# Nineteen weight units whose low part is completed by an accumulating DMA instead of a VectorE subtraction

## The chip, the cores and the metric

The kernel runs on one core of a Trainium2 chip. The metric is device time in microseconds, the median of several executions. Engines: PE (TensorE matmul), PEld (its weight loads), DVE (VectorE), ACT (ScalarE), POOL (GpSimd) and SP (SyncE), which issues nearly all DMAs.

## What is computed

One layer of a hybrid decoder trunk on 512 tokens of width 2048, all in float32:

```
h    = rms_norm(x, norm1_g)
proj = h @ w_in            # columns: aq ak av | bu bg | cq ck cv
out_a = dilated mixture of attentions (8 heads x 64)         from aq, ak, av
out_b = silu(layer_norm(causal depthwise conv(bu * sigmoid(bg))))
out_c = sliding-window grouped-query attention with sinks (16 heads x 64) from cq, ck, cv
x    = x + concat(out_a, out_b, out_c) @ w_out
h2   = rms_norm(x, norm2_g)
x    = x + (silu(h2 @ w_gate) * (h2 @ w_up)) @ w_down
```

q and k are normalised per head before the attentions.

## The kernel before

**Matmuls in three parts.** A float32 operand is split into a high part, rounded to the fp32r type, and a low part, the operand less its high part, in fp32r too. A product is then three matmuls that add up in PSUM (`mm3`, lines 321 to 324): high weights by high activations (322), high weights by low activations (323), low weights by high activations (324). Activations are kept as pairs `hh`, `hl`; weights as pairs `wh`, `wl`.

**Weight units.** Weights arrive in units of 128 partitions by 1024 columns (512 KB). The input projection takes units 0 to 62: units 0 to 10 belong to the first four projections, worked together, and from unit 11 on each further projection of the list `PROJ` takes two units, an odd one and then an even one (`project`). Units 63 to 94 are `w_out`; the FFN follows with other blocks. A unit's 8 slices of 128 columns take 24 matmuls of 512 columns.

**From the raw unit to the pair.** `pump` issues the loads on SP (line 243) into a few raw buffers, in order, as they come free. `next_unit` is called when a unit's matmuls are about to be written down; it calls `split_up_to(u + 2)`, so a unit is split two units ahead of its use. In the projections the split is a cast on ACT (line 289, raw to `wh`) and a subtraction on DVE (line 263, raw less `wh` gives `wl`). The subtraction is not written down at once but kept in the list `lows` and written down after the fourth slice of the unit in progress (`lows_now` in `project`). `wh` and `wl` have three buffers each (`SPLIT_BUFS`), so the cast of unit u waits until PE has read the high part of unit u-3 for the last time, which is about when unit u-2 begins.

**Release of raw buffers.** While the projections run (`cooling`), a raw buffer that was split goes to the list `cool`; `lows_now` moves the lists on (`release`) and calls `pump`, but only where `lows` holds something. A buffer is thus given back one and a half units after its split.

**The work around it.** Everything beside the projections' matmuls (convolution, heads' normalisation, attention) is placed by a hand-made clock: `ticks.tick()` is called after every second slice, and each step is due some ticks after the one before. Instructions of an engine run in the order in which they are written down, each waiting for what it reads. POOL's queue in this stage holds, among others: the product of the gated linear unit (line 573), the power steps that make the scales of q and k (lines 664 to 666), the scaling of v by the norm (773), and the triangular masks that spread the attention's turned probabilities, high and low (`spread_out`, lines 906 and 909, tiles `c..ph` and `c..pl`). PE reads those masks' results in `weigh` (lines 974 and 975). ACT's queue holds, besides the casts of the weights, the exponentials, the copies of PSUM and the high parts of activations (for example `c..hp`, line 892, and `av`, line 779); DVE's the taps of the convolution (582), the low parts and the reductions.

## Time and profile before

| | |
|---|---|
| median of 3 runs | 1841.37 us (1841.23 to 1842.32) |
| profiled execution | 1840.9 us, span 1839.1 us, granted PE clock 1.00 |
| busy: PE, PEld, DVE, ACT, POOL | 1832.4, 1522.4, 1428.2, 1312.8, 1018.3 us |
| DMA | 337.81 MB, mean 184 GB/s, queue q1 takes 62.3% of 16 engines |
| stage with the changed units | 100 to 345 us of the span |

The profile is one execution. Times in its rows are from the start of the span. A row of the timeline has start, duration, engine, line, operation, the tile written and the tiles read (buffer numbers left out), the shape, and in brackets how long the engine had been idle and what ended that. A PE duration is modelled and overlaps the next one; matmuls of 512 columns start about 0.23 us apart. DMA issues show on the issuing engine's queue (SPq).

### The profile page before, as it was taken

What the parts mean: (1) busy time and instruction counts of PE and PEld (TensorE: products, weight loads), DVE (VectorE), ACT (ScalarE), POOL (GpSimd) and SP (SyncE); (2) the same over time, 40 slices, a digit from 0 to 9 for tenths busy, and PEclk for the clock granted to TensorE, in tenths of its full rate; (3) what the DMA queues carried; (4) which work ended last, traced back from release to release, by engine and by line L of the source; (5) the groups of instructions that cost most, each with busy time, mean ns of one, the idle gap of its engine ahead of it and who ended that gap; (6) DMA issues with size and microseconds to landing.
All of it is one profiled execution on the core that took longest, in us unless ns stands there. A gap on an engine that the chain in (4) does not pass through costs nothing.

```text
span 1839.1 us, 26573 instructions
## 1 busy us (share of the span) xinstructions
PE 1832.4 (100%) x8319; PEld 1522.4 (83%) x8319; DVE 1428.2 (78%) x2024; ACT 1312.8 (71%) x1784; POOL 1018.3 (55%) x793
## 2 busy tenths in 40 slices
PE   9999999999999999999999999999999999999998
PEld 7888888888888888888888888888888888888887
DVE  7689888986689877777777777777777777777777
ACT  6355644553468788888888888888887778877775
POOL 0126544110003557886888767887776558776552
PEclk9999999999999999999999999999999999999999
DMA  7353255453343466777867777677687579877635
GB/s 277 89 149 122 88 144 156 111 174 120 132 138 106 113 162 182 206 206 185 223 177 211 207 185 224 175 205 208 182 271 258 199 233 283 266 255 258 237 120 109
DMA packets 401612, 337.81 MB, mean 184 GB/s; under 512 B 185408, under 2 KB 327872, under 8 KB 401472
## 3 DMA queue, kind: packets, MB, share of 16 engines
q1 hardware_dynamic: 400896, 335.33, 62.3%
q8 instruction: 66, 1.08, 0.3%
q10 hardware_dynamic: 576, 0.79, 0.1%
q14 instruction: 74, 0.61, 0.1%
HBM read 261.61 MB, written 66.03 MB: 178 GB/s over the span
## 4 chain that ended last, share of the span: by engine, by line
PE 99%; DVE 1%; DMA 0%; issue 0%; SPq 0%; ACT 0%; DVEq 0%
PE out L1315 15%; PE out L1313 15%; PE out L1316 15%; PE out L1578 7%; PE out L1579 7%; PE out L1580 7%; PE o L324 3%; PE o L323 3%; PE o L322 3%; PE cq L322 2%; PE cq L324 2%; PE cq L323 2%; PE aq L322 1%; PE ak L322 1%; PE av L322 1%; PE aq L324 1%
## 5 line engine op out<-in xcount | busy, mean ns | idle before, releaser
L1313 PE MATMUL out<-wh,h 128*128 128x512 f32 x1232 | 479.2, 389 | 0.0
L1315 PE MATMUL out<-wl,h 128*128 128x512 f32 x1232 | 479.2, 389 | 0.0
L1316 PE MATMUL out<-wh,h 128*128 128x512 f32 x1232 | 479.2, 389 | 0.0
L1313 PEld LDWEIGHTS out<-wh,h 128*128 128x128 f32 x1232 | 231.3, 188 | 48.0
L1316 PEld LDWEIGHTS out<-wh,h 128*128 128x128 f32 x1232 | 231.3, 188 | 48.0
L1315 PEld LDWEIGHTS out<-wl,h 128*128 128x128 f32 x1232 | 231.3, 188 | 47.8
L1578 PE MATMUL out<-wh,a 128*128 128x512 f32 x620 | 240.4, 388 | 0.0
L1579 PE MATMUL out<-wl,a 128*128 128x512 f32 x620 | 240.3, 388 | 0.0
L1580 PE MATMUL out<-wh,a 128*128 128x512 f32 x620 | 240.3, 388 | 0.0
L289 ACT CAST wh<-w 128x1024 fp32r<-128x1024 f32 (+2 forms) x94 | 96.9, 1031 | 138.6 <-PE o L323 49.3
L1588 DVE TENSOR_TENSOR y<-y,out 128x512 f32<-128x512 f32 x192 | 128.3, 684 | 45.4 <-PE out L1580 43.8
L263 DVE TENSOR_TENSOR wl<-w,wh 128x1024 fp32r<-128x1024 f32 (+2 forms) x95 | 114.3, 1204 | 33.5 <-ACT wh L289 33.2
L1578 PEld LDWEIGHTS out<-wh,a 128*128 128x128 f32 x620 | 116.4, 188 | 24.0
L1579 PEld LDWEIGHTS out<-wl,a 128*128 128x128 f32 x620 | 116.4, 188 | 23.8
L1580 PEld LDWEIGHTS out<-wh,a 128*128 128x128 f32 x620 | 116.4, 188 | 23.8
L582 DVE SCALAR_TENSOR_TENSOR y<-bu,cst,y 128x511 f32<-128x511 f32 (+14 forms) x120 | 89.7, 747 | 1.1
L322 PE MATMUL o<-mh_c,wh 128*128 128x512 f32 x128 | 51.0, 399 | 0.0
L322 PE MATMUL cq<-hh,wh 128*128 128x512 f32 x128 | 50.3, 393 | 0.0
L324 PE MATMUL o<-mh_c,wl 128*128 128x512 f32 x128 | 50.0, 391 | 0.0
L323 PE MATMUL o<-ml_c,wh 128*128 128x512 f32 x128 | 50.0, 390 | 0.0
L323 PE MATMUL cq<-hl,wh 128*128 128x512 f32 x128 | 49.9, 390 | 0.0
L324 PE MATMUL cq<-hh,wl 128*128 128x512 f32 x128 | 49.9, 390 | 0.0
(2357 smaller groups left out, 4741.5 us busy)
## 6 DMA issues: line engine op xcount, KB each, us to landing
od<-a SPq DMA_DIRECT2D x154, 256.0 KB
a<-od SPq DMA_DIRECT2D x154, 256.0 KB
w<-in_wi SPq DMA_DIRECT2D x58, 512.0 KB
w<-in_wo SPq DMA_DIRECT2D x32, 512.0 KB
x<-in_xT SPq DMA_DIRECT2D x16, 256.0 KB
xr<-in_xT SPq DMA_DIRECT2D x16, 256.0 KB
x2d<-xr SPq DMA_DIRECT2D x16, 256.0 KB
z<-x2d SPq DMA_DIRECT2D x64, 64.0 KB
```

What stands on the lines that cost most here:

```text
L263: fn(*args)
L289: (nc.vector.tensor_copy if u == 0 else nc.scalar.copy)(hi[:, :n], t[:, :n])
L322: nc.tensor.matmul(out, wh, xh, start=start, stop=False)
L323: nc.tensor.matmul(out, wh, xl, start=False, stop=False)
L324: nc.tensor.matmul(out, wl, xh, start=False, stop=stop)
L1313: nc.tensor.matmul(b, x[:, high], wh[:, s], start=c == f == 0 and q in (7, 1, 5, 2), stop=False, skip_group_check=True)
L1315: nc.tensor.matmul(b, x[:, high], wl[:, s], start=False, stop=False, skip_group_check=True)
L1316: nc.tensor.matmul(b, x[:, low], wh[:, s], start=False, stop=c == f == 1, skip_group_check=True)
L1578: nc.tensor.matmul(b[:, lo:hi], x[:, high], wh[:, s], start=start, stop=False, skip_group_check=True)
L1579: nc.tensor.matmul(b[:, lo:hi], x[:, high], wl[:, s], start=False, stop=False, skip_group_check=True)
L1580: nc.tensor.matmul(b[:, lo:hi], x[:, low], wh[:, s], start=False, stop=last, skip_group_check=True)
L1588: getattr(eng, op)(t, t, src)
```

## The change

For the units of a fixed set, every second one from 21 to 57 (which is 19 units: the first half of each projection from cq1 to aq2 in the order of `PROJ`), the subtraction on DVE is left out. ACT writes the negative of the raw unit, rounded to fp32r, into `wl` right after the cast into `wh`; then a DMA issued from POOL's queue reads the unit from DRAM once more and adds it to `wl` in place. The sum is the raw unit less its high part, as before. The list `lows` gets no entry for such a unit, so nothing is written down for it after the fourth slice, and the release of raw buffers and the loads that follow it happen there only for the other units. Where `lows` is empty after the split, `next_unit` calls `pump` itself.

```
+LOWS_BY_DMA = set(range(21, 58, 2))
...
+    def complete(lo, u, n):
+        nc.gpsimd.dma_start(lo[:, :n], units[u], accum_op=ALU.add)
...
                 (nc.vector.tensor_copy if u == 0 else nc.scalar.copy)(hi[:, :n], t[:, :n])
-                lows.append((eng.tensor_sub, lo[:, :n], t[:, :n], hi[:, :n].bitcast(F32)))
+                if u in LOWS_BY_DMA:
+                    nc.scalar.activation(lo[:, :n], t[:, :n], AF.Copy, scale=-1.0)
+                    complete(lo, u, n)
+                else:
+                    lows.append((eng.tensor_sub, lo[:, :n], t[:, :n], hi[:, :n].bitcast(F32)))
                 if not late_lows:
                     lows_now()
```

## Prediction

> **What bounds the kernel now.** I read the head of the page first, then the chain that ended last, then the engines' busy times over the stage that the change touches (100 to 345 us), and last the waits of the PE instructions that read what other engines made there.

> ```profile
> span 1839.1 us, 26573 instructions
> ...
> PE 1832.4 (100%) x8319; PEld 1522.4 (83%) x8319; DVE 1428.2 (78%) x2024; ACT 1312.8 (71%) x1784; POOL 1018.3 (55%) x793
> ...
> PE 99%; DVE 1%; DMA 0%; issue 0%; SPq 0%; ACT 0%; DVEq 0%
> ```
> ```profile
> 100.00:345.00 245.00, 245.00 (x1247) 207.71 (x1246) 212.59 (x439) 130.01 (x285) 106.26 (x172) 1.00 0.44 125
> ```
> The reader is to see that the end is set by PE alone: 99% of the chain, and in the stage PE is busy 245 of 245 us at a granted clock of 1.00. The columns after the window are PE, PEld, DVE, ACT, POOL, clock, DMA share, GB/s. DVE has 87% there, ACT 53%, POOL 43%: three engines that feed PE and are never late by more than the following row of the "sat idle until" list of the c4o matmuls (line 975) admits. That row is the only wait of a PE instruction on another engine that I found in this stage.

> ```profile
>   POOL c4pl L909: 0.2, 1
> ```
> So work taken from DVE is worth at most about 0.2 us here: nothing that PE waits for is late because of DVE. What the change can do is make something late. The question is only how much.

> **The change, part by part.** It touches units 21, 23, ... 57: 19 units (the first halves of the projections from cq1 to aq2).

> *DVE.* Removed: 19 subtractions at 1.224 us (median of the row below), 23.3 us of DVE time in a stage where DVE is not on the chain. Worth 0.

> ```profile
> L263 DVE TENSOR_TENSOR wl<-w,wh x39: 1189/1224/1439, 90.1 to 342.4; 128x1024 fp32r<-128x1024 f32 x39
> ```
> *ACT.* Added: one more pass over 128x1024, right behind the cast of the same unit and as long as it (1.05 us): 19 x 1.05 = 20 us. It is hidden by ACT's idle 115 us; what stands behind it comes 1.0 us later at most, until the next gap. If that cover were gone, each would cost up to 1.05 us.

> *SP.* The raw buffers are released only where a subtraction is pending, so now once in two units, and the loads of the stage are issued one unit (odd) or two units (even) later in program order, past whatever SP issues in between. They had about 5.5 units of lead, and keep 3.5. A unit lasts some 6.1 to 6.7 us (the casts of 128.27 and 141.73 below are two units apart, and so are those of 265.06 and 277.35), so 21 us stay. A plain load of 512 KB takes 3.0 us: issued at 171.95, all of it moved by 174.9.

> ```profile
> 171.95 0.36 SPq L243 DMA_DIRECT2D w<-in_wi  x1
> ```
> ```profile
> 172.90:174.90 2.00, 2.00 (x10) 1.65 (x9) 1.79 (x5) 1.99 (x5) 1.84 (x4) 1.00 0.74 262
> 174.90:176.00 1.10, 1.10 (x6) 0.93 (x5) 1.07 (x3) 1.10 (x7) 1.10 (x2) 1.00 0.00 0
> ```
> 262 GB/s for 2.0 us is 524 KB; before that, 1.0 us passes from the issue. Cost 0, and 10 MB more are read in 240 us that move 125 GB/s; also 0.

> *The landing of the accumulating DMA.* No row shows one. The lower bound is the plain load's 3.0 us. For the upper one I let the moving take four times as long (source read, destination read, add, write): 1.0 + 8.0 = 9.0 us. I take twice, 5.0 us, since what is read doubles and nothing else is known to. Against this stands the time from the issue to PE's first use of wl. The tightest unit is 21:

> ```profile
> 92.51 1.06 ACT L289 CAST wh<-w 128x1024 fp32r<-128x1024 f32 x1 [4.38 <-PE bu L323]
> ```
> ```profile
> 103.87 0.39 PE L324 MATMUL cq<-hh,wl 128*128 128x512 f32 x1
> ```
> The cast ends at 93.57; an ACT pass that follows directly starts 0.10 us earlier (next fence: 128.27 + 1.05, next start 129.22), so the negative copy ends at 93.57 + 0.95 = 94.52. With 1.5 us for the issue (below) 7.85 us remain until 103.87. 5.0 us fits; only above 7.85 us does any PE instruction wait, and in the other eighteen, worked out the same way, 8.0 to 12.1 us remain. Cost 0.

> *POOL's queue.* This is where I see a cost. POOL now holds an instruction that waits for ACT's negative copy, which waits for the cast, which waits for a buffer that PE frees only when unit u-2 begins. Until now POOL ran ahead of that. Behind it stand POOL's next instructions: the products of the power steps (line 664 on), glu, the scaling of v (773), and the masks of the probabilities (906, 909), which PE's lines 974 and 975 read. And the issue itself takes POOL some time g. No row shows a DMA issued by POOL: the nearest below is SP's issue of such a load, 0.43 us in the median; the nearest above is POOL's longest pass here, 2.66 us (144.44). POOL's own ordinary 128x512 pass takes 1.04 us (263.61). I take g = 1.5, the middle of the two ends and close to that pass.

> ```profile
> L243 SPq DMA_DIRECT2D w<-in_wi x42: 333/430/593, 65.6 to 330.6; - x42
> ```
> I went through all 19 places: end of the negative copy plus g, against the start of the POOL instruction behind it, and that shift against the slack of its reader. At fifteen PE waits for nothing: POOL stood still (waiting for a DMA), or the reader comes later than the shift; at units 41 and 51 DVE, not PE, would wait, by under 1 us. Four remain.

> Unit 27 (ACT, POOL, PE):
> ```profile
> 128.27 1.05 ACT L289 CAST wh<-w 128x1024 fp32r<-128x1024 f32 x1
> 129.22 0.59 ACT L892 CAST c0hp<-c0t 128x512 fp32r<-128x512 f32 x1
> ...
> 129.70 0.20 POOL L664 TENSOR_TENSOR cq1r<-cq1t 128x8 f32<-128x8 f32 x1 [11.83 <-DMA cq1t<-cq1d]
> ...
> 136.96 1.27 POOL L909 TENSOR_SCALAR_AFFINE_SELECT c0pl<-c0lp 128x128 fp32r<-128x128 f32 x1
> ...
> 140.03 0.28 PE L975 MATMUL c0o<-c0pl,cv 128*128 128x256 f32 x1
> ```
> The negative copy ends at 129.32 + 0.95 = 130.27, POOL is free at 131.77, 2.07 later than 129.70. POOL works without a gap from there to 138.23; PE reads at 140.03, slack 1.80 (rounded starts). **0.3 us.**

> Unit 29:
> ```profile
> 141.73 1.05 ACT L289 CAST wh<-w 128x1024 fp32r<-128x1024 f32 x1 [0.63 <-PE bu L323]
> ...
> 138.43 0.61 POOL L906 TENSOR_SCALAR_AFFINE_SELECT c0ph<-c0hp 128x256 fp32r<-128x256 f32 x1 [0.20 <-ACT c0hp L892]
> ...
> 139.71 0.79 POOL L909 TENSOR_SCALAR_AFFINE_SELECT c0ph<-c0hp 128x128 fp32r<-128x128 f32 x1
> 143.28 0.84 POOL L906 TENSOR_SCALAR_AFFINE_SELECT c0pl<-c0lp 128x256 fp32r<-128x256 f32 x1 [2.78 <-DVE c0lp L897]
> ...
> 144.44 2.66 POOL L906 TENSOR_SCALAR_AFFINE_SELECT c0pl<-c0lp 128x256 fp32r<-128x256 f32 x1
> 147.06 0.73 POOL L909 TENSOR_SCALAR_AFFINE_SELECT c0pl<-c0lp 128x128 fp32r<-128x128 f32 x1
> ...
> 150.53 0.28 PE L975 MATMUL c0o<-c0pl,cv 128*128 128x256 f32 x1
> ```
> Free at 142.78 + 0.95 + 1.5 = 145.23, where c0ph stood at 138.43; its four passes (2.07 us) end at 147.30, so c0pl starts 4.02 late; it ended at 147.78 and is read at 150.53, slack 2.75. **1.3 us.**

> Unit 47:
> ```profile
> 265.06 1.05 ACT L289 CAST wh<-w 128x1024 fp32r<-128x1024 f32 x1
> 266.00 0.71 ACT L779 CAST av<-av0s 128x256 fp32r<-128x256 f32 x2
> ...
> 263.61 1.04 POOL L773 TENSOR_TENSOR av0s<-av0s,n1w 128x512 f32<-128x512 f32 x1 [13.05 <-DMA ak0e<-ak0wide]
> ...
> 271.04 0.83 POOL L906 TENSOR_SCALAR_AFFINE_SELECT c4pl<-c4lp 128x256 fp32r<-128x256 f32 x1 [0.15 <-DVE c4lp L897]
> ...
> 273.97 0.70 POOL L909 TENSOR_SCALAR_AFFINE_SELECT c4pl<-c4lp 128x128 fp32r<-128x128 f32 x1
> ...
> 276.75 0.28 PE L975 MATMUL c4o<-c4pl,cv 128*128 128x256 f32 x1
> ```
> av0s starts at 266.11 + 0.95 + 1.5 = 268.56 and ends at 269.60. ACT reads it at 266.00, so ACT itself stands for 3.6 us, and with it the passes behind, down to c4hp, which POOL's c4ph needs. The shift at c4pl is 3.6 - 0.15; it ended at 274.67, read at 276.75, slack 2.08. **1.4 us.**

> Unit 49:
> ```profile
> 277.35 1.05 ACT L289 CAST wh<-w 128x1024 fp32r<-128x1024 f32 x1
> ...
> 277.36 0.41 POOL L906 TENSOR_SCALAR_AFFINE_SELECT c4ph<-c4hp 128x256 fp32r<-128x256 f32 x1 [2.68 <-PE c4o L975]
> ...
> 280.61 1.96 POOL L666 TENSOR_TENSOR cq6r<-cq6r,nhalf 128x8 f32<-128x8 f32 x1
> 284.97 0.60 POOL L906 TENSOR_SCALAR_AFFINE_SELECT c4pl<-c4lp 128x256 fp32r<-128x256 f32 x1 [2.40 <-PE c6s L852]
> ...
> 286.69 0.29 POOL L909 TENSOR_SCALAR_AFFINE_SELECT c4pl<-c4lp 128x128 fp32r<-128x128 f32 x1
> ...
> 287.03 0.38 PE L975 MATMUL c4o<-c4pl,cv 128*128 128x256 f32 x1
> ```
> Free at 278.40 + 0.95 + 1.5 = 280.85 instead of 277.36, so cq6r ends at 282.57 + 3.5 = 286.07, and c4pl starts 1.1 late with a slack of 0.05. **1.0 us.**

> Sum: 0.3 + 1.3 + 1.4 + 1.0 = 4.0 us. PE has no idle in which to win a stall back, so each lands at the end. By the same steps g = 0.43 gives 0.2 + 0.35 = 0.6 us, and g = 2.66 gives 1.4 + 2.4 + 2.6 + 2.2 = 8.6 us.

> [...]

> The profiled execution took 1840.9 us (span 1839.1 and 1.8 us around it), 0.5 us below the median of 1841.37. Made there the sum is 1844.9; on the median **1845.4 us**.

> **The rivals.**

> *Hidden after all (no change).* DVE's subtraction slows POOL while it runs: the pass of 2.66 us stands beside the one at 144.97, and the same kind of pass took 0.41 at 277.36. The subtractions of units 27, 29 and 49 fall on the very chains above; with them gone those passes may shrink. Recovering 1 us at each of the three leaves 0 + 0.3 + 1.4 + 0 = 1.7 us: 1843.1. It decides as soon as POOL gets back 0.3 us of the 4.0. Against it: the chains are shifted onto other DVE work, and DVE stays 77% busy (212.6 less 23.3, of 245). The same outcome follows from g below 1.4.

> ```profile
> 144.97 1.21 DVE L263 TENSOR_TENSOR wl<-w,wh 128x1024 fp32r<-128x1024 f32 x1
> ```
> *The issue starved.* If POOL's writing of the issue is held up beside DVE as that mask pass was (2.66 against 0.41), g is at its upper end everywhere: +8.6, 1850.0. DVE stands at 87% in the stage, which speaks for it; against it, one such pass in four of that chain was held, not all. [...]

> *The landing late.* If the accumulating DMA takes 10 us from its issue, seven of the nineteen units are late by 0.4 to 2.1 us and three by less, 10.8 us together: with POOL's 4.0, 1856. At 12 us it is about 40. For it: the stage's other traffic holds 44% of the DMA engines and two loads are now issued at a time. Against it: it needs more than three times the plain load.

> *Faster.* Needs a PE wait that DVE causes; the stage has 0.2 us of waits in all.

> **How the numbers follow.** 0.2% (3.7 us) is about what a measurement of this kernel can tell from no change, so 1845.05 is the border. The forecast (small stalls behind POOL's queue, 3.7 to 8 us) has 0.42; hidden, 0.36; issue starved, 0.07; landing late, 0.13; faster, 0.02. Slower over 0.2% is then 0.42 x 0.95 + 0.07 + 0.13 = 0.60; the 0.05 falls within the border by scatter: same 0.38, faster 0.02. The range starts at the lowest sum less the scatter shown (1841.4 + 0.6 - 0.7 = 1841.3, put at 1841.0) and reaches to the landing of 10 us (1857); outside are faster (0.02) and landings beyond 10 us (0.08).

> **What would show it.** Right: DVE's line 263 has 19 fewer, ACT 20 us more, PE's lines 974 and 975 wait for POOL's c0pl and c4pl by about 1 us each, and PE's wl matmuls wait for no DMA. Wrong: waits of PE for a DMA into wl (landing late), no PE wait over 0.3 us (hidden), or a POOL row for the issue outside 0.4 to 2.7 us, and then the sum moves by about 4 us for each us of it.

## The result and the profile after

The kernel after takes **1845.26 us** in the median of 15 runs (1844.16 to 1851.15), the kernel before, run beside it, 1841.23 us (1840.67 to 1842.32). By the medians it is slower by 4.0 us. The ratio, 1.0028 with a 95% interval of 1.002 to 1.0036, follows the means, which four runs of 1849 to 1851 us pull up. In the kernel after, the lines below 263 stand 2 to 9 further down: the subtraction is line 265, the new DMA issue line 270, ACT's cast 294, its new negative copy 296, the masks 915 and 918, and PE's reads of them 983 and 984.

The page of the kernel after (engine, busy us, share, instructions; then a costly group with count, busy, mean ns and idle time ahead; then the DMA issue with the median us to its landing):

```profile
span 1843.3 us, 26611 instructions
...
PE 1833.3 (99%) x8319; PEld 1521.9 (83%) x8319; DVE 1410.7 (77%) x2005; ACT 1330.4 (72%) x1803; POOL 1029.3 (56%) x812
...
L270 POOL DMA_DIRECT2D wl<-in_wi x19 | 17.2, 906 | 97.3 <-ACT wl L296 96.8
...
wl<-in_wi POOLq DMA_DIRECT2D x19, 512.0 KB, 5.5
```

PE does the same 8319 matmuls in nearly the same busy time (1833.3 against 1832.4 us); the span grew by 4.2 us. So most of the loss is idle time of PE. The list of PE's waits names it (what waited, for what: total us, times, longest):

```profile
PE c4o L984 <- POOL c4pl L918: 1.4, 2, 1.1
...
PE cq L333 <- DMA wl<-in_wi: 0.4, 1, 0.4
PE in L331 <- ACT wh L294: 0.4, 1, 0.4
PE c0s L862 <- DMA ckl<-cklo: 0.3, 1, 0.3
```

None of these four waits of PE is in the profile before (the 0.2 us for c4pl that the prediction shows is idle time of PEld, ahead of a weight load). A wait's length is not yet its cost, because the matmuls around it lose some overlap (between c4pl's two waits, rows of 0.28 us start 0.12 us apart). For the cost I took the start of the k-th matmul in both traces and looked where the difference grows: +0.88 us in the first 10 us, +0.70 at 105.3 (the first matmul that reads unit 21's wl), +0.62 at 108.3 (c0s), +1.64 at 289.8 to 290.8 (c4pl). That is 3.84 us; at the last matmul it is 3.74.

The largest of the four, in the timeline of the kernel after (start, length, engine, line; in brackets idle time and what ended it):

```profile
279.92 1.05 ACT L294 CAST wh<-w 128x1024 fp32r<-128x1024 f32 x1
280.87 1.06 ACT L296 ACTIVATE wl<-w 128x1024 fp32r<-128x1024 f32 x1
...
282.23 0.89 POOL L270 DMA_DIRECT2D wl<-in_wi  x1 [5.25 <-ACT wl L296]
282.81 0.78 POOL L915 TENSOR_SCALAR_AFFINE_SELECT c4ph<-c4hp 128x256 fp32r<-128x256 f32 x1
...
286.42 2.57 POOL L675 TENSOR_TENSOR cq6r<-cq6r,nhalf 128x8 f32<-128x8 f32 x1
288.96 0.40 POOL L915 TENSOR_SCALAR_AFFINE_SELECT c4pl<-c4lp 128x256 fp32r<-128x256 f32 x1
...
289.78 0.39 PE L984 MATMUL c4o<-c4pl,cv 128*128 128x256 f32 x1 [1.11 <-POOL c4pl L918]
```

POOL stands at unit 49's issue until ACT's negative copy ends at 281.93. The four masks of c4ph stand behind it, behind them cq6r, behind that the masks of c4pl, for which PE waits.

### The profile page after: what moved, and what is told of

Its sections match the earlier page's. It is cut to its first block, busy times and chain, and to the rows that moved or that the text cites. A ratio compares the mean times of both kernels' runs of the same rounds, so it can differ in the third digit from the quotient of the medians.

```text
span 1843.3 us, 26611 instructions
## 1 busy us (share of the span) xinstructions
PE 1833.3 (99%) x8319; PEld 1521.9 (83%) x8319; DVE 1410.7 (77%) x2005; ACT 1330.4 (72%) x1803; POOL 1029.3 (56%) x812
## 4 chain that ended last, share of the span: by engine, by line
PE 83%; DVE 1%; issue 0%; DMA 0%; POOL 0%; ACT 0%; DVEq 0%
PE out L1324 15%; PE out L1322 15%; PE out L1325 15%; PE out L1587 7%; PE out L1589 7%; PE out L1588 7%; PE o L333 3%; PE o L332 3%; PE o L331 3%; PE aq L331 1%; PE aq L333 1%; PE aq L332 1%; PE av L331 1%; PE av L333 1%; PE av L332 1%; DVE y L1597 0%
## 5 line engine op out<-in xcount | busy, mean ns | idle before, releaser
L265 DVE TENSOR_TENSOR wl<-w,wh 128x1024 fp32r<-128x1024 f32 (+2 forms) x76 | 91.1, 1200 | 23.4 <-ACT wh L294 22.0
L270 POOL DMA_DIRECT2D wl<-in_wi x19 | 17.2, 906 | 97.3 <-ACT wl L296 96.8
```

The lines of the kernel that those rows point to most:

```text
L265: fn(*args)
```

## The experiments

Each kernel ran beside the kernel before, on the same chip. Where an edit is to "the changed kernel", it starts from the kernel after.

**Controls.** The kernel before and the changed kernel again, without an edit.

> The kernel before, unchanged, as a control for runs of one program against itself. Every theory: ratio 1.000 within 0.0006. What it tells: in the profile of the changed kernel PE is 0.9 us late already at 10 us of the span (the first wait of PE for a cast, 0.4 us), before anything that was changed. Theory A (start-up scatter from the first loads): this profile's PE differs from the first profile of the same kernel by some tenths of a us in the first 10 us too. Theory B (the POOL-issued DMA queue costs start-up time): this profile starts as the first one did, within 0.1 us.

> The changed kernel once more, unchanged. Theory A (waits at fixed places): +3 to +4 us, ratio 1.0015 to 1.0025; PE waits again for c4pl at about 290 us (1.6 us in shift) and for the landing of the first accumulating DMA at about 105 us (0.3 to 0.9), and nowhere else by over 0.3 us after the start-up. Theory B (scatter of the landings): the places change from one profile to the next.

Before: 1841.29 us (1840.82 to 1841.58) against 1841.20, ratio 1.0001 (0.9992 to 1.0009). After: 1844.81 us (1843.73 to 1850.32), ratio 1.0024 (1.0014 to 1.0035). The second profile of the changed kernel has c4pl again, to within 0.01 us (+1.65 us), but not the other small losses: nothing at the start, nothing for unit 21, and more for the c twin.

```profile
PE c4o L984 <- POOL c4pl L918: 1.4, 2, 1.1
...
PE c0s L862 <- DMA ckl<-cklo: 0.8, 1, 0.8
```

So one of the losses is fixed and the others come and go. The two profiles of the kernel before differ by 0.004 us at the last matmul. Its unprofiled runs scatter too, though (1840.68 to 1843.42 us in the 26 beside these), so some of the scatter need not come from the change.

**Two of the places given back to DVE.**

```
-LOWS_BY_DMA = set(range(21, 58, 2))
+LOWS_BY_DMA = set(range(21, 58, 2)) - {21, 49}
```

> The changed kernel, with units 21 and 49 split on DVE as before; the other 17 keep the accumulating DMA. Theory A (two places alone cost: the first landing among the loads and the k twins at 96 to 108 us, and POOL's hold before c4pl at 290 us): the waits for wl, for ckl and for c4pl go, and the time falls to that of before plus 0 to 1 us, ratio 1.0000 to 1.0006. Theory B (a cost spread over all units, or of having the queue at all): 17/19 of the loss stays, ratio about 1.002.

1842.71 us (1841.07 to 1844.86), ratio 1.0008 (1.0000 to 1.0017). The waits at 105 to 108 us and for c4pl are gone, and with them some 2.1 us of the median. What is left, 1.5 us, lies between the two theories' forecasts. Part of it is new, a wait at 328.4 us (the 0.8 us for `wh` is at the start):

```profile
PE c6o L984 <- POOL c6pl L918: 0.9, 1, 0.9
PE in L331 <- ACT wh L294: 0.8, 1, 0.8
```

**The raw buffers released for every unit**, as in the kernel before, where the changed kernel releases only where a subtraction is pending:

```
-    def lows_now():
-        if lows and cooling:
+    def lows_now(every=False):
+        if (lows or every) and cooling:
...
-                    lows_now()
+                    lows_now(True)
```

> The changed kernel with the raw buffers given back after the fourth slice of every unit, as before the change, so that the loads are issued one by one again and not two at a time. Theory A (the later, paired loads cost nothing): ratio as the changed kernel's, 1.0015 to 1.0025, with the wait for c4pl unchanged (1.6 us). Theory B (the loads in pairs crowd the DMA engines and delay the first landing): the waits at 105 to 108 us, 1.3 us in shift, go, and the ratio falls to about 1.001.

A miss for both theories: 1852.98 us (1846.24 to 1855.73), ratio 1.0060 (1.0048 to 1.0073). In its profile PE waits far longer at known places:

```profile
PE c4o L984 <- POOL c4pl L918: 5.2, 2, 4.2
PE c0s L861 <- DMA ckh<-ckhi: 2.0, 1, 2.0
```

At c4pl, POOL now stands 6.76 us for cq6t, the head scales' small round trip through DRAM, and c4pl stands behind it; the accumulating DMAs land after 7.1 us in the median instead of 5.5. At c0s, the raw loads on SP ahead of the twins (small copies of k that the attention reads) tell more. The same place in the kernel before, the changed kernel and this one:

```profile
95.36 1.52 SPq L243 DMA_DIRECT2D w<-in_wi  x3
```
```profile
96.06 1.05 SPq L245 DMA_DIRECT2D w<-in_wi  x2
```
```profile
95.52 1.54 SPq L245 DMA_DIRECT2D w<-in_wi  x3
```

With one load more some 2 us ahead of them in all three, four raw loads go out there in the kernel before and in this one, three in the changed kernel. Four without unit 21's DMA cost PE nothing, three with it 0.3 and 0.8 us of waiting (the two profiles of the changed kernel), four with it 2.0.

And a wait costs more than itself. The windows around the c0s wait (window, length, busy PE, PEld, DVE, ACT, POOL with counts, granted clock, DMA share, GB/s):

```profile
105.00:108.00 3.00, 1.83 (x8) 1.13 (x7) 1.06 (x2) 2.98 (x5) 0.92 (x1) 1.00 1.09 236
...
110.00:112.00 2.00, 2.00 (x7) 1.71 (x7) 1.20 (x5) 0.00 (x0) 0.00 (x0) 0.50 1.06 237
```

The granted clock falls to 0.50 for 6.83 us as this wait ends, and for 6.83 us again within the one of 4.2 us. Matmuls of 512 columns start 0.43 us apart there instead of 0.23. Behind the first wait PE falls back by another 3.6 us (a further wait of 0.4 us included), behind the second by 2.3: over a third of this profile's 14.8 us. So when the loads are issued matters, as the theories did not have it, and for this kernel the later ones are the better. Why c4pl is so much later with the single loads was not separated further, and no run has the later loads without any DMA from POOL.

**The issue a little later.** The DMAs are kept in a list and written down where the pending subtractions are; the order of POOL's queue changes at seven units (29, 33, 35, 37, 41, 49, 55), where the issue stood directly ahead of masks or of the product of the gated linear unit, and now stands behind them.

```
-                    complete(lo, u, n)
+                    late_dmas.append((lo, u, n))
...
+        while late_dmas: complete(*late_dmas.pop(0))     # in lows_now, after the lows
```

> The changed kernel with every accumulating DMA issued a little later in the program: GpSimd's queue order differs only where an issue now stands behind mask or add passes instead of ahead of them (at unit 49 behind the four c4ph passes). Theory A (GpSimd's queue is in order: at unit 49 the issue, which waits for ScalarE's negative copy, holds the c4ph and c4pl passes): TensorE's wait for c4pl, 1.4 us in the changed kernel's profile, falls under 0.4 us, the waits for c0s's twins and unit 21's landing stay, median 1843.4 us (ratio about 1.0012). Rival B (c4pl is late because the extra transfers delay the loads ahead of it): the wait for c4pl stays at 1.0 us or more and the median at 1844.5 to 1845.5. Rival C (an issue later by some us makes the landing late): new waits of TensorE for wl by DMA, median over 1846.

On the mechanism theory A holds: with c4ph ahead of unit 49's issue, PE waits no more for c4pl (the shift there is 0.0 us, against 1.64 and 1.65). c4pl starts as early against PE as in the kernel before (PE is 2.06 us behind it here, and 287.03 less 2.06 is 284.97), although cq6r's last pass takes 2.65 us here. ACT's copy (280.38) comes only 0.4 us earlier against PE than in the changed kernel, so it is the order that counts:

```profile
277.67 0.76 POOL L915 TENSOR_SCALAR_AFFINE_SELECT c4ph<-c4hp 128x256 fp32r<-128x256 f32 x1
...
280.38 1.06 ACT L296 ACTIVATE wl<-w 128x1024 fp32r<-128x1024 f32 x1
281.74 0.88 POOL L270 DMA_DIRECT2D wl<-in_wi  x1 [2.33 <-ACT wl L296]
...
287.03 0.60 POOL L915 TENSOR_SCALAR_AFFINE_SELECT c4pl<-c4lp 128x256 fp32r<-128x256 f32 x1 [0.81 <-PE c6s L861]
...
288.50 0.39 PE L984 MATMUL c4o<-c4pl,cv 128*128 128x256 f32 x1
```

The time is none of those expected for A or B, and rival C's number came by another way than its landings: 1848.20 us (5 runs, 1843.82 to 1850.34), ratio 1.0033 (1.0020 to 1.0046). The place at 329 us, known from the run without units 21 and 49, is back and larger:

```profile
PE c6o L984 <- POOL c6pl L918: 2.0, 1, 2.0
...
PE cq L333 <- DMA wl<-in_wi: 0.6, 1, 0.6
```

and again the clock fell behind it, for 3.41 us. The moved issue of unit 55 does not hold c6pl: the first two c6pl masks run right behind it (323.64 and 324.00), and it is the third that stands, for 3.46 us until 328.15.

**The hold without the bytes.** DVE keeps all subtractions, so that the raw loads go out one at a time as in the kernel before; ACT's negative copy goes to a tile of its own, and POOL accumulates into that.

```
-                    nc.scalar.activation(lo[:, :n], t[:, :n], AF.Copy, scale=-1.0)
-                    complete(lo, u, n)
-                else:
-                    lows.append((eng.tensor_sub, ...))
+                    aside = wp.tile([P, T], F32R, ...)
+                    for half in range(2):
+                        nc.scalar.activation(aside, t[:, half * T:half * T + T], AF.Copy, scale=-1.0)
+                    nc.gpsimd.dma_start(aside[:, :16], units[u][:, :16], accum_op=ALU.add)
+                lows.append((eng.tensor_sub, ...))
```

> VectorE still makes every low part; ScalarE's negative copy goes to a tile of its own that TensorE never reads, in two passes, and GpSimd issues an accumulating DMA of 8 KB instead of 512 KB into it. So it has the wait and the issue in GpSimd's queue but almost no transfer, and no late landing. Theory A (the hold): TensorE still waits 1 to 2.5 us for c4pl at unit 49, possibly 0.7 us for c0pl at unit 29 since VectorE is as busy as before; no wait for ckl or wl; median 1843.0 to 1844.5 us. Rival B (transfers): no wait for c4pl, median 1841.2 to 1841.7.

1841.95 us (1841.20 to 1843.20) against 1841.44, ratio 1.0003 (0.9994 to 1.0011): theory A's number missed. POOL is held at unit 49 as before, but c4pl just makes it:

```profile
278.38 1.30 ACT L298 ACTIVATE wa<-w 128x512 fp32r<-128x512 f32 x2
...
280.56 0.79 POOL L916 TENSOR_SCALAR_AFFINE_SELECT c4ph<-c4hp 128x256 fp32r<-128x256 f32 x1
...
284.19 1.67 POOL L676 TENSOR_TENSOR cq6r<-cq6r,nhalf 128x8 f32<-128x8 f32 x1
285.83 0.40 POOL L916 TENSOR_SCALAR_AFFINE_SELECT c4pl<-c4lp 128x256 fp32r<-128x256 f32 x1
```

Two things are earlier than in the changed kernel. From the first c4ph mask to the first of c4pl it takes 5.27 us here, 6.15 there: the cq6r pass takes 1.67 us and not 2.57. And the issue comes 0.70 us earlier against PE (279.97 with PE 0.60 behind the kernel before, 282.23 with PE 2.16 behind); a copy of ACT ahead of the cast waits 0.29 us there instead of 1.22. Together that is 1.6 us, the whole stall. So the hold is needed for that stall, as the later issue shows, but it is not enough: c4pl lies on an edge on which tenths of a us decide. Whether the bytes, the idle DVE or the later loads took those tenths in the changed kernel, this run does not tell, as it changes all three.

**The same with 256 KB** (512 columns instead of 16).

> As the kernel with the 8 KB transfer beside VectorE's low parts, but the accumulating DMA moves 256 KB (512 columns) into the tile that TensorE never reads. Wait and issue in GpSimd's queue are the same; only the bytes grow. Theory A' (the loss needs the hold and the crowding of transfers together): median 1842.5 to 1844 us, and in the profile a wait of 0.3 us or more for a c twin's load or for c4pl or c6pl. Rival (the hold alone, bytes do not count): 1841.9 us as with 8 KB, no wait of TensorE.

1842.57 us (1841.12 to 1843.77) against 1841.10, ratio 1.0006 (0.9997 to 1.0015). The profile is of its shortest run and shows no wait in the stage; what its longer runs wait for was not seen. Not decided, though the scatter with bytes (2.65 us) lies above that with 8 KB (2.0).

**The accumulation left out.**

```
-        nc.gpsimd.dma_start(lo[:, :n], units[u], accum_op=ALU.add)
+        nc.gpsimd.dma_start(lo[:, :n], units[u])
```

> The changed kernel with the accumulation left out: the same 512 KB go from the same source to the same tile by the same queue, and overwrite the negative copy, so TensorE multiplies by the raw unit as its low part. If plain bytes crowd the other transfers: landing 4 to 5.5 us and the same waits, median 1844 to 1845.5 us. If the accumulation's read of the tile in SBUF is what crowds: landing 3 to 4 us (a raw unit's load took 3.0 us in the profile before), no wait for unit 21 and the c twin, median 1842 to 1843.5 us.

1843.82 us (1842.60 to 1847.85) against 1841.10, ratio 1.0015 (1.0007 to 1.0024). It lands earlier, and PE waits only for c4pl:

```profile
PE c4o L984 <- POOL c4pl L918: 1.4, 2, 1.1
...
wl<-in_wi POOLq DMA_DIRECT2D x19, 512.0 KB, 4.3
```

So neither reading was right alone: plain bytes leave 2.7 of the 4 us in the median, and c4pl is 1.65 of the profile. The accumulation lands 1.2 us later in the median. Whether it carries the waits for unit 21 and the c twin is not shown: the profile is of the shortest run (1842.60 us), and in the changed kernel too these waits come and go.

**ACT's part alone.** The negative copy stays, DVE adds the raw unit.

```
-                    complete(lo, u, n)
+                    lows.append((nc.vector.tensor_add, lo[:, :n], lo[:, :n].bitcast(F32), t[:, :n]))
```

> ScalarE's negative copy stays, but VectorE adds the raw unit onto it in place of the DMA: ScalarE's part of the change alone, with no software DMA and VectorE as busy as before. The low part has the other sign in neither: it is raw minus rounded only in the changed kernel's sense of raw added to the copy. Theories A and B: ScalarE's 20 us are hidden, median 1841.0 to 1841.8 us, no wait of TensorE for c4pl, ckl or wl. Rival D (ScalarE's longer stretch delays its c4hp and exp passes): waits of TensorE for c4pl or for ScalarE, median 1842.5 or more.

1841.87 us (1841.45 to 1842.37) against 1841.44, ratio 1.0001 (0.9992 to 1.0010). ACT's passes are hidden, to within about half a us (the profile has one new wait in the stage, 0.3 us for c1pl).

**One DMA alone**, `LOWS_BY_DMA = {57}`.

> Only unit 57, the last of the nineteen, gets its low part by the accumulating DMA; the other eighteen are as before. It tells whether one software DMA anywhere brings the scatter at the start (0 to 1.9 us, a second x load that lands later) seen in the kernels with nineteen. If it does: runs spread from 1841 to 1843 us with a median of 1841.6 to 1842.3. If the scatter needs something else: median 1841.0 to 1841.4 with the spread of the kernel before (1840.7 to 1841.9). In both, unit 57 itself costs nothing.

1841.12 us (1840.86 to 1841.74), ratio 0.9999 (0.9990 to 1.0008). One DMA issued by POOL does not bring the scatter at the start. Its cause stays open.

**Three places given back to DVE**, `LOWS_BY_DMA = set(range(21, 58, 2)) - {21, 49, 55}`.

> Units 21, 49 and 55 stay with VectorE, the other sixteen with the DMA. Theory A' (the loss sits at these three places): TensorE waits for none of ckl, wl, c4pl, c6pl for more than 0.3 us, median 1841.3 to 1842.2 us. Rival (the waits move to other units as the schedule shifts): another wait of 0.7 us or more, median 1842.7 us or more as without units 21 and 49.

1841.48 us (1841.11 to 1842.46) against 1841.10, ratio 1.0001 (0.9992 to 1.0010): the other sixteen of the nineteen units cost 0.4 us in the median, which these runs do not tell from nothing. So the loss does sit at these places. But the wait at 328 us did not need unit 55's DMA, and there theory A' missed. The profile, of the longest run, still has it:

```profile
PE c6o L984 <- POOL c6pl L918: 0.8, 1, 0.8
```

The third c6pl mask there stands 3.13 us until 326.01. Ahead of it, SP issues the ak1 twins late (first the kernel before, then this one):

```profile
309.31 0.51 SPq L243 DMA_DIRECT2D w<-in_wi  x1
311.60 1.12 SPq L752 DMA_DIRECT2D ak1h<-ak1hi  x2
```
```profile
313.67 0.97 SPq L245 DMA_DIRECT2D w<-in_wi  x2
314.74 1.12 SPq L761 DMA_DIRECT2D ak1h<-ak1hi  x2
```

SP issues its small transfers in the same order in these two profiles and in the changed kernel's, among them round trips through DRAM, whose way back waits for the way out to land (av1s for av1d: SP stands 0.6 us for it in the kernel before, 1.2 us in the changed one). At this point PE is 0.34 us behind the kernel before, SP 3.1 us, and two raw loads have just been issued together ahead of the twins. The mask waits with the twins in flight. In the changed kernel's profile the same mask waits too, without a loss, and there the end of the wait is put down to a twin:

```profile
327.42 0.41 POOL L915 TENSOR_SCALAR_AFFINE_SELECT c6pl<-c6lp 128x256 fp32r<-128x256 f32 x1 [1.40 <-DMA ak1l<-ak1lo]
```

That the mask waits for the twins' buffer is my reading of the program; no run tests it.

**A longer hold.** Two passes more on POOL behind unit 49's issue.

```
                     complete(lo, u, n)
+                    if u == 49:
+                        aside = wp.tile([P, T], F32, ...)
+                        nc.gpsimd.memset(aside, 0.0)
+                        nc.gpsimd.tensor_add(aside, aside, aside)
```

> The changed kernel with two more passes on GpSimd (a memset and an addition, 128 by 512 each, some 1.5 us) right behind the issue of unit 49. TensorE's wait for c4pl grows from 1.4 to about 3 us. If a wait of over 2 us also halves TensorE's clock, as in the two profiles with such waits (3.4 to 6.8 us at 0.5 afterwards, 1.7 to 3.4 us lost): median 1848 to 1850.5 us, where the runs of 1849 to 1851 us of the changed kernel lie. If it costs only its own length: 1846 to 1847 us.

1847.19 us (5 runs, 1845.98 to 1849.79), ratio 1.0033 (1.0020 to 1.0046): between the two. In the profile, of the longest run, both happened:

```profile
PE c6o L988 <- POOL c6pl L922: 2.8, 1, 2.8
PE c4o L988 <- POOL c4pl L922: 2.7, 2, 2.4
```
```profile
290.00:292.00 2.00, 1.69 (x10) 1.37 (x11) 0.66 (x1) 0.54 (x1) 0.82 (x2) 1.00 0.72 229
...
333.00:336.00 3.00, 3.00 (x9) 2.32 (x8) 2.90 (x10) 1.89 (x4) 0.00 (x0) 0.50 0.23 40
```

After the wait of 2.4 us the granted clock stayed at 1.00; after the one of 2.8 us it was 0.50 for 3.41 us. So here a wait of 2 to 3 us may or may not cost the clock; how the waits lay in each case, the last section shows.

## Why the prediction was right, and where it was not

**The total.** 1845.4 us was forecast, 1845.26 measured, well inside the range. That closeness is mostly luck. Of the four stalls on POOL's queue, 4.0 us together, only unit 49's came, with 1.64 us for 1.0. Of the other 2.2 us in the profile, 1.32 came from steps costed at nothing (unit 21's landing and the c twin) and 0.88 from the start of the kernel, which the change does not touch. Of the prediction's own signs, the waits for c0pl did not come, and PE did wait for a DMA into wl, which it had named as a sign against itself.

**PE the bound, nothing to win from DVE.** Right. DVE does 19 subtractions fewer and nothing got faster; PE is 99% busy before and after.

**ACT hidden.** Right: 17.6 us more on ACT, and by itself about 0.4 us from the kernel before (ACT's part alone).

**POOL's queue.** The mechanism was right at unit 49 (the later issue takes the stall away). Two things went wrong elsewhere. First the size: the term g was 1.5 us. The issue's row is 0.91 us, the next instruction starts 0.6 us after the issue's start, and the issue starts 0.3 us after the copy's end, so POOL is free about 0.9 us after the copy. At unit 27 the smaller g alone takes the stall away: the shift is then 1.5 us, within the slack of 1.80.

Second the order: at units 29 and 47 the prediction put the issue on the wrong side of its neighbours in POOL's queue. At unit 29 it let c0ph's masks stand behind the issue. They stand ahead of it, and only c0pl's are held:

```profile
142.11 0.73 POOL L918 TENSOR_SCALAR_AFFINE_SELECT c0ph<-c0hp 128x128 fp32r<-128x128 f32 x1
...
146.20 0.92 POOL L270 DMA_DIRECT2D wl<-in_wi  x1 [3.36 <-ACT wl L296]
...
148.32 0.40 POOL L915 TENSOR_SCALAR_AFFINE_SELECT c0pl<-c0lp 128x256 fp32r<-128x256 f32 x1
...
152.21 0.28 PE L984 MATMUL c0o<-c0pl,cv 128*128 128x256 f32 x1
```

By the prediction's own rows c0pl then starts 145.23 - 143.28 = 1.95 us late and not 4.02, within the slack of 2.75: no stall, even with g = 1.5. In the trace c0pl is done 3.2 us before PE reads it. At unit 47 the prediction let av0s wait behind the issue, and ACT behind av0s. But av0s stands ahead of the issue:

```profile
267.89 1.04 POOL L782 TENSOR_TENSOR av0s<-av0s,n1w 128x512 f32<-128x512 f32 x1 [8.69 <-DMA av0s<-av0d]
...
269.46 0.91 POOL L270 DMA_DIRECT2D wl<-in_wi  x1 [0.54 <-DMA w<-in_wi]
...
276.69 0.29 POOL L918 TENSOR_SCALAR_AFFINE_SELECT c4pl<-c4lp 128x128 fp32r<-128x128 f32 x1
...
278.42 0.28 PE L984 MATMUL c4o<-c4pl,cv 128*128 128x256 f32 x1
```

So ACT is later by its own negative copy alone, c4pl's first mask by 1.0 us against PE and not by 3.4, and c4pl ends 1.4 us before its reader (276.98 against 278.42).

The rival that passes on POOL shrink where a subtraction goes is right as an observation: the pass of 2.66 us at unit 29 is one of 0.40, and it is 2.66 again in the run in which DVE adds there. It was not needed: with DVE's subtraction and POOL's hold together (the 8 KB run) PE does not wait for c0pl either.

At unit 49 the smaller g alone would have made c4pl 0.5 us late against a slack of 0.05. It is 1.8 us late against PE: ACT's cast comes 0.4 us later, and POOL takes 6.15 us from the first c4ph mask to the first of c4pl, against 5.21 in the kernel before up to the end of cq6r. The four c4ph masks take 3.07 us there instead of 1.34, the three cq6r passes 3.08 instead of 3.87. Why the masks are slower was not separated.

**The landing.** 5.0 us was taken, 5.5 is the median, so this term was well sized; the step that failed is the use of one number for all units. Unit 21, which I named as the tightest with 7.85 us left, took 9.6:

```profile
95.72 1.06 POOL L270 DMA_DIRECT2D wl<-in_wi  x1 [5.04 <-ACT wl L296]
...
105.33 0.50 PE L333 MATMUL cq<-hh,wl 128*128 128x512 f32 x1 [0.43 <-DMA wl<-in_wi]
```

Three raw loads (one issued at 93.8 us, two from 96.1) and then the c twins were issued around it. The mean over the stage before (44% of the DMA engines, 125 GB/s) hid that from 95 to 105 us the engines were at 85% already; in the kernel after they are at 96%.

**SP's loads, cost 0.** This failed. The raw units themselves stayed early enough; what I left out is the small transfers on SP behind the bytes. The c twin cost 0.62 and 1.05 us in the two profiles of the changed kernel. There the rows point to the second reading of unit 21 and not to the pairing of the loads, as fewer raw loads are issued around it than before. The late c6pl, which I put down to the ak1 twins, cost 1.0 to 2.9 us in four variants and nothing in the changed kernel's two profiles.

**The issue starved.** It did not come: the 19 issues take 0.86 to 1.06 us beside a DVE that is busy for 193.0 of the stage's 245 us.

**Still open:** the scatter at the start (0 to 1.9 us, a load of x that lands late), and the runs of 1849 to 1851 us of the changed kernel, 4 of 15 here. A wait past 2 us with one lapse of the clock would add up to that, by an estimate from the waits seen (2.0 to 2.8 us, and 1.7 us for 3.41 us at 0.50), and their mean granted clock is 0.998. But a run of 1845.85 us has 0.998 too, and no profile fell on one of the four.

## What to carry to other kernels

Work taken off an engine that nothing waits for is worth nothing (here 17.5 us of DVE's busy time), and its replacement has to be paid in queues: look at what stands behind the instruction that now waits, on every in-order queue, and at what its bytes push aside in the fullest 10 us, not in the mean of the stage. Take the order of a queue from the program, not from the times at which its instructions ran before: two of the four stalls here were forecast on the wrong side of the issue. Price a landing by its slowest case against the tightest reader. And a stall of TensorE of about 2 us or more may cost double: four of the five such waits seen here (2.04 to 4.19 us) came with a granted clock of 0.50 for 3.41 or 6.83 us, and behind the one of 2.05 us PE fell back by another 3.6 us, a further wait of 0.4 us included.
